# Convolution taps accumulated in a PSUM bank that the attention's side work shares, in a hybrid encoder block

## The chip, the cores and the metric

The kernel runs on one core of a Trainium2 chip. The metric is the time of one execution on the device in microseconds (us), the median of several runs. Engines are named as in the profile: PE multiplies matrices, DVE is the vector engine, ACT the scalar engine, POOL the GpSimd engine, SP issues DMAs. Each engine works through its own queue in program order. SBUF is the large on-chip memory; PSUM is the small one that PE writes into, 8 banks of 512 fp32 columns on 128 partitions.

## What is computed

The input is 1024 tokens of 1024 channels, all fp32. Cut to what matters here:

```python
h = rmsnorm(x, norm1_g); p = h @ w_in            # q | k | v | value | gate
q, k = rope(rmsnorm(q)), rope(rmsnorm(k))        # 8 query heads, 2 key heads, 64 wide
attn = softmax(q k^T / 8) v
c = value * sigmoid(gate)                        # 512 channels
c = depthwise_conv(c, conv_dw, width=31) + conv_b
conv = silu(layernorm(c))
x = x + concat(attn, conv) @ w_out
out = rmsnorm(x + peer(rmsnorm(x)))              # 16384 experts, top 16 of 8 heads
```

## The kernel before

Everything up to the output projection takes the first 591 us and is what the change touches; the expert part (`peer`) fills the rest of the span and is untouched. An order written out by hand (`manual_schedule`) fixes each engine's queue: instructions run on an engine in the order in which the Python code emits them. Matrix products are made of three products of split operands (`split` on L114, `mm3` on L121: the high part is cast on ACT, the low part is a subtraction on DVE or POOL).

**Stage A** (to L484) makes Q, K, V and the gated convolution input `hp`. The convolution's 512 channels are four tiles c of 128 channels; the 1024 tokens are two halves th. For each (c, th), `ag_mm` (L252) makes the gate (k=1) and then the value (k=0), each 24 matmuls into one half of a PSUM tile of two banks, of which there are two; `ag_sg` (L260) applies the sigmoid on ACT, and `ag_mul` (L265) writes the product into `hp` on DVE. The other four banks (tag `t`) serve the transposes and the projections of K, V (`kv_mm`) and Q (`q_mm`). The order is c = 3, then 0 and 1, then K and V for eight token tiles, Q for eight token tiles, then c = 2.

**The taps.** The convolution has 31 taps. A pass takes one tile c and 512 tokens: a first step multiplies by the first tap and adds the bias, and 30 more steps add one tap each. On DVE (`taps_v`, L141) a step is one instruction that reads `hp` shifted by w, multiplies by the tap's column and adds to `y`, in place in SBUF. On POOL (`taps_p`, L149) a step multiplies into a tile `cm` (on ACT in stage A, on POOL in the attention, switch `alone`) and adds it to `y`. The passes are generators in two queues, `ct_v` and `ct_p`; `adv(n)` emits the next n steps. The places of these calls and the constants CV1 to CV3, CP1, CP3, AV0, AV1, AP0, AP1 set how many taps stand between the other instructions. DVE takes the passes of tiles 3 and 1 and the second half of 2, POOL those of tile 0 and the first half of 2.

**The attention** (L492 to L816) has 64 units, one for each of 8 token tiles and 8 heads. The loop on L761 emits for each unit u, in the order of ORD: both halves of the transposed probabilities (`p_tr`, tile ptP, split into PT), the next exponential (`s_exp`), scores two units ahead (`s_mm`) and their maximum (`s_max`, L697, one per unit: it serves as the unit's clock), every fourth unit the transposed queries (`qt_make`, ql and qh), every second unit the product with V (`pv`) and the fold and scaling (`pfold`, L741 to L744, into `mo`). Then come taps of both queues.

Side work goes into slots of this loop: when the 8 heads of a token tile are done, its output projection (`outproj`, L590) is queued: 4 transposes, a split, and for each half of the columns 12 + 12 matmuls and an addition to X, 8 steps in all. When all passes of a token half are done, its layernorm (`layernorm_steps`, L506) is queued, and goes first. `slot("c")`, `slot("p")` and `slot("q")` each emit the current item's next step if it is of that kind; one item is worked on at a time, and all of them use one PSUM bank (`side_bank`, tag `x`). What is left at the end of the loop is emitted behind it (L803 to L815), step by step without other work, and then `outproj_conv` (L607) adds the convolution's part: PE products pwo<-PT and additions on L616.

Of the kernel before, what the change touches and what calls it, by code (L numbers as in the profile page):

```python
# [53 lines left out]
AV1 = 2  # L54
AV0 = 1
# [7 lines left out]
CP1 = 3  # L63
CP3 = 2
AP1 = 1
AP0 = 2
CV1 = 6
CV2 = 3
CV3 = 6


def peer_block(tc, I, out):
# [54 lines left out]
    with ExitStack() as fr:  # L127
# [10 lines left out]
        cm_ = fr.enter_context(tc.tile_pool(name="cm", bufs=1))  # L138
        hp = [None] * NCT

        def taps_v(c, o):  # L141
            yo = y[c][:, o:o + 512]
            V.tensor_scalar(yo, hp[c][:, o:o + 512], cw[:, c, 0:1], cvec[:, 0, c:c + 1], op0=ALU.mult, op1=ALU.add)
            yield
            for w in range(1, CW):
                V.scalar_tensor_tensor(yo, hp[c][:, w + o:w + o + 512], cw[:, c, w:w + 1], yo, op0=ALU.mult, op1=ALU.add)  # L146
                yield

        def taps_p(c, o):  # L149
            yo = y[c][:, o:o + 512]  # L150
            G.tensor_scalar(yo, hp[c][:, o:o + 512], cw[:, c, 0:1], cvec[:, 0, c:c + 1], op0=ALU.mult, op1=ALU.add)
            yield
            for w in range(1, CW):
                m = cm_.tile([P, 512], F32, name="cm", tag="cm", bufs=2)
                src = hp[c][:, w + o:w + o + 512]
                if alone["on"]:
                    G.tensor_scalar(m[:], src, cw[:, c, w:w + 1], 0.0, op0=ALU.mult, op1=ALU.add)
                else:
                    A.activation(m[:], src, AF.Copy, scale=cw[:, c, w:w + 1])
                G.tensor_tensor(yo, yo, m[:], op=ALU.add)  # L160
                yield

        alone = dict(on=False)
# [17 lines left out]
        left = {(c, o) for c in range(NCT) for o in (0, 512)}  # L181

        with ExitStack() as st:
# [68 lines left out]
            def ag_mm(c, th, k):  # L252
                if k == 1:
                    PA[c, th] = ps.tile([P, 2, 512], F32, name="pa", tag="big", bufs=2)
                w = WAG[k * NCT + c]
                for dc in range(DC):
                    mm3(PA[c, th][:, k, :], w[0][:, dc, :], w[1][:, dc, :],
                        hT(0, dc, th * 512, 512), hT(1, dc, th * 512, 512), dc == 0, dc == DC - 1)

            def ag_sg(c, th):  # L260
                sg = y[2][:, th * 512:(th + 1) * 512]
                A.activation(sg, PA[c, th][:, 1, :], AF.Sigmoid)
                PA[c, th] = (PA[c, th], sg)

            def ag_mul(c, th):  # L265
                pa, sg = PA.pop((c, th))
# [4 lines left out]
                V.tensor_tensor(hp[c][:, PAD + th * 512:PAD + (th + 1) * 512], pa[:, 0, :], sg, op=ALU.mult)  # L271
# [104 lines left out]
            ag_mm(3, 0, 1)  # L376
            prep_b(4)
# [5 lines left out]
            ag_sg(3, 0)  # L383
# [4 lines left out]
            ag_mm(3, 1, 1)  # L388
            wsplit_ag(4, G)
            ag_mm(3, 1, 0)  # L390
            ag_sg(3, 1)
# [3 lines left out]
            for o in (0, 512):  # L395
                ct_v.add(taps_v(3, o), (3, o))
            for c in (0, 1):
                for th in range(2):
                    for k in (1, 0):
# [7 lines left out]
                        ct_v.adv(1)  # L407
                        if k == 0:
                            ag_sg(c, th)
                            ag_mul(c, th)  # L410
                        ct_v.adv(CV1 - 1)
                        ct_p.adv(CP1 - th)
                WAG.pop(c), WAG.pop(c + 4)
                if c == 0:
                    for o in (0, 512):
                        ct_p.add(taps_p(0, o), (0, o))
                else:
                    ct_v.add(taps_v(1, 0), (1, 0), True)
                    ct_v.add(taps_v(1, 512), (1, 512))
# [27 lines left out]
            for t in range(NT):  # L447
# [6 lines left out]
                else:  # L454
                    qa(t - 1)
                    ct_v.adv(CV2)
                if t == 1:
# [10 lines left out]
            for th in range(2):  # L468
                for k in (1, 0):
# [6 lines left out]
                    if k == 0:  # L476
                        ag_sg(2, th)
                        ag_mul(2, th)
                    if th == 0 or k == 1:
                        ct_v.adv(CV3)  # L480
                    if th == 0:
                        ct_p.adv(CP3)
            ct_p.add(taps_p(2, 0), (2, 0), True)
            ct_v.add(taps_v(2, 512), (2, 512))  # L484
# [7 lines left out]
        with ExitStack() as st:  # L492
# [3 lines left out]

            def side_bank(name):
# [1199 lines left out]
```

## Time and profile before

| | us |
|---|---|
| runs of the kernel | 3000.25, 3005.8, 3015.49 |
| median | 3005.8 |
| the profiled execution | 3001.72 |
| its span, first to last instruction | 2999.9 |

The profiled execution's time is that of the whole execution; its span is 1.8 us shorter. In the rows below, a tile is named without its buffer number, out<-in; "x5" is a number of instructions merged into one row, and the time of such a row runs from the first one's start to the last one's end. The releaser in brackets is inferred, and "issue" means that the profile shows none. `L119` and `L122` to `L124` are lines of the helpers `split` and `mm3`, so the tile's name says what they work for.

### The profile page before, as it was taken

The numbers are of one execution on the slowest core, as the hardware profiler recorded it, in microseconds if no ns is written. First come the engines' busy times: TensorE is split into PE (matmuls) and PEld (weight loads), VectorE is DVE, ScalarE is ACT, GpSimd is POOL, SyncE is SP. The second block draws the span as 40 slices with busy tenths as digits, with TensorE's granted clock in tenths as the row PEclk, the third lists the DMA queues.
The fourth block names the chain that finished last, engine by engine and source line by source line (L and its number), as shares of the span: only waits on it lengthen the run. The fifth ranks groups of instructions, "written<-read, shape, count | busy, mean of one in ns | idle before, by whom it ended". The sixth has DMA issues, their size and how long they took to land.

```text
span 2999.9 us, 44538 instructions
## 1 busy us (share of the span) xinstructions
PE 2796.1 (93%) x16048; PEld 2476.5 (83%) x16048; DVE 2464.3 (82%) x4465; ACT 1148.3 (38%) x2376; POOL 1951.2 (65%) x1557
## 2 busy tenths in 40 slices
PE   7878899899999899988999999999999999999997
PEld 6767778699978788867888888888888888888886
DVE  5888998457667867874999988898999999899898
ACT  3216566243577577673222222222222222222222
POOL 2577842104445757774777777777777777777775
PEclk9999999999999999999999999999999999999999
DMA  3111000044334567576889898999899999999896
GB/s 125 51 68 36 8 1 15 31 145 131 109 122 163 205 245 265 196 288 246 340 330 344 328 347 334 339 337 355 335 338 335 354 342 340 339 339 340 331 343 230
DMA packets 296720, 710.33 MB, mean 237 GB/s; under 512 B 25265, under 2 KB 135217, under 8 KB 296369
## 3 DMA queue, kind: packets, MB, share of 16 engines
q0 software_dynamic: 110592, 402.70, 35.1%
q1 hardware_dynamic: 156800, 252.85, 25.0%
q10 hardware_dynamic: 29104, 51.91, 4.6%
q8 instruction: 126, 2.06, 0.3%
q14 instruction: 98, 0.79, 0.1%
HBM read 640.46 MB, written 66.91 MB: 236 GB/s over the span
## 4 chain that ended last, share of the span: by engine, by line
PE 50%; DVE 21%; DMA 12%; issue 8%; POOL 4%; ACT 4%; ACTq 1%; SPq 0%; POOLq 0%; DVEq 0%
PE hps L1492 12%; PE hps L1234 5%; PE prot L122 4%; PE prot L123 3%; PE prot L124 3%; DMA rows<-peer_u,ei 3%; DMA vr<-peer_v 3%; DVE y L146 3%; PE pg L1098 3%; DMA rows<-peer_v,ei 3%; DVE ga L1197 2%; PE acc L122 2%; PE acc L124 2%; PE acc L123 2%; DVE ho L1475 2%
## 5 line engine op out<-in xcount | busy, mean ns | idle before, releaser
L1492 PE MATMUL hps<-HN,uh 128*128 128x320 f32 x3072 | 682.9, 310 | 9.9 <-ACT ho L1241 5.3
L1492 PEld LDWEIGHTS hps<-HN,uh 128*128 128x128 f32 x3072 | 530.3, 188 | 42.9 <-issue 5.5
L1492 PE MATMUL hps<-HN,ul 128*128 128x320 f32 x1536 | 476.1, 310 | 0.6 <-POOL ul L119 0.6
L1197 DVE SCALAR_TENSOR_TENSOR ga<-rows,aa,ga 128x1024 f32<-128x1024 f32 x330 | 423.9, 1285 | 23.3 <-DMA rows<-peer_v,ei 16.7
L1152 POOL DMA_INDIRECT rows<-peer_u,ei x339 | 360.3, 1063 | 109.5 <-issue 57.9
L119 POOL TENSOR_TENSOR vl<-vr,vh 128x1024 fp32r<-128x1024 f32 x128 | 308.9, 2413 | 154.0 <-ACT vh L116 110.8
L1152 POOL DMA_INDIRECT rows<-peer_v,ei x330 | 325.4, 986 | 110.6 <-issue 64.1
L1185 DVE SCALAR_TENSOR_TENSOR QB<-rows,ga 128x1024 bf16<-128x1024 f32 x271 | 329.5, 1216 | 30.0 <-DMA rows<-peer_u,ei 25.8
L122 PE MATMUL prot<-vh,ah 128*128 128x512 f32 x762 | 308.3, 405 | 29.2 <-DVE X L1557 26.9
L119 POOL TENSOR_TENSOR ul<-ur,uh 128x1024 fp32r<-128x1024 f32 x127 | 323.2, 2545 | 2.6
L1557 DVE TENSOR_TENSOR X<-X,prot 128x512 f32<-128x512 f32 x384 | 262.0, 682 | 68.1 <-PE prot L124 66.7
L123 PE MATMUL prot<-vl,ah 128*128 128x512 f32 x762 | 301.2, 395 | 0.4 <-POOL vl L119 0.4
L124 PE MATMUL prot<-vh,al 128*128 128x512 f32 x762 | 297.6, 390 | 0.0
L1492 PEld LDWEIGHTS hps<-HN,ul 128*128 128x128 f32 x1536 | 289.2, 188 | 0.9 <-POOL ul L119 0.9
L1502 ACT ACTIVATE ho<-hps 128x320 f32<-128x320 f32 x128 | 55.8, 436 | 486.4 <-PE hps L1492 486.4
L1108 ACT COPY gblk<-pg 128x128 f32<-128x128 f32 x640 | 175.9, 441 | 97.0 <-PE pg L1098 72.5
L116 ACT CAST vh<-vr 128x1024 fp32r<-128x1024 f32 x128 | 133.7, 1045 | 202.1 <-DMA vr<-peer_v 193.3
L1234 PE MATMUL hps<-HN,uh 128*128 128x320 f32 x992 | 210.0, 334 | 0.0
L124 PE MATMUL acc<-vh,al 128*128 128x512 f32 x512 | 199.6, 390 | 0.0
L122 PE MATMUL acc<-vh,ah 128*128 128x512 f32 x512 | 199.6, 390 | 0.0
L123 PE MATMUL acc<-vl,ah 128*128 128x512 f32 x512 | 199.5, 390 | 0.0
L122 PEld LDWEIGHTS prot<-vh,ah 128*128 128x128 f32 x762 | 143.3, 188 | 64.6 <-DVE X L1557 44.5
(270 smaller groups left out, 6556.6 us busy)
## 6 DMA issues: line engine op xcount, KB each, us to landing
ur<-peer_uT SPq DMA_DIRECT2D x128, 512.0 KB, 4.2
vr<-peer_v SPq DMA_DIRECT2D x128, 512.0 KB, 7.8
GD<-gblk ACTq DMA_DIRECT2D x80, 512.0 KB, 5.2
gl<-GD SPq DMA_DIRECT2D x64, 640.0 KB, 8.0
wqr<-peer_wq SPq DMA_DIRECT2D x32, 512.0 KB, 3.9
HDm<-ho SPq DMA_DIRECT2D x31, 320.0 KB, 2.6
s<-SD SPq DMA_DIRECT2D x64, 128.0 KB, 2.9
ho<-HDm SPq DMA_DIRECT2D x22, 320.0 KB, 4.6
```

The source lines that it names most:

```text
L116: A.copy(hi, src)
L119: lo_eng.tensor_tensor(lo, src, f(hi), op=ALU.subtract)
L122: PE.matmul(ps, ah, bh, start=start, stop=False)
L123: PE.matmul(ps, ah, bl, start=False, stop=False)
L124: PE.matmul(ps, al, bh, start=False, stop=stop)
L1108: A.copy(gblk[b][k][:, :, q * 4:q * 4 + 4].rearrange("p i t -> p t i"), pg[:, :, k * w:k * w + w])
L1152: G.indirect_dma_start(out=r, out_offset=None, in_=I["peer_v" if ph else "peer_u"], in_offset=bass.IndirectOffsetOnAxis(ap=ge[t][:, k:k + ...
L1185: V.scalar_tensor_tensor(jk, r, 1.0, h, op0=ALU.mult, op1=ALU.mult, accum_out=self.hh[t][:, k:k + 1])
L1197: V.scalar_tensor_tensor(to, r, self.aa[t][:, k:k + 1], to, op0=ALU.mult, op1=ALU.add)
L1234: PE.matmul(hps[:, j, :b - a], (uh, uh, ul)[st3][:, dc, :], HN[(0, 1, 0)[st3]][:, dc, a:b], start=dc == 0 and st3 == 0, stop=dc == DC - 1 ...
L1492: PE.matmul(ps[:, :b - a], (uh, uh, ul)[st3][:, dc, :], HN[(0, 1, 0)[st3]][:, dc, a:b], start=dc == 0 and st3 == 0, stop=dc == DC - 1 and ...
L1557: V.tensor_tensor(X[:, NG + t, n:n + 512], X[:, NG + t, n:n + 512], pr, op=ALU.add)
```

## The change

The taps of DVE accumulate in a PSUM tile `ac` instead of `y`; only the last tap writes `y`. The bank for it comes from a new pool `psT` that lives through stage A and the attention, and it is the bank of the side work (layernorm and output projection). In stage A the gate and the value each get a bank of their own, three in rotation, in place of two tiles of two banks; the sigmoid is emitted right behind the gate's matmuls. POOL multiplies and adds its taps alone everywhere, none on ACT. The second half of tile 0 is divided: tokens 512 to 767 stay on POOL, 768 to 1023 go to DVE. The numbers of steps per place change. In the attention each unit gets two steps of each queue; the slots take up no side work until DVE's queue of taps is empty, and from then on, while more than one item waits, the order ORD2 gives a unit two "p" and two "c" slots. The result of a unit goes into the columns of Q that it has used, not into a tile of its own.

```diff
@@ -51,8 +51,8 @@
 ORD = "c01esmdqvpf"
-AV1 = 2
-AV0 = 1
+ORD2 = "c01pesmdcqvpf"
+AV0 = 2
 GQ = 4
@@ -60,13 +60,13 @@
 RH = 4
-CP1 = 3
-CP3 = 2
-AP1 = 1
+CP1 = 2
+CP2 = 1
+CP3 = 1
 AP0 = 2
-CV1 = 6
-CV2 = 3
-CV3 = 6
+CV1 = 7
+CV2 = 4
+CV3 = 5
@@ -136,31 +136,31 @@
         cm_ = fr.enter_context(tc.tile_pool(name="cm", bufs=1))
+        psT = fr.enter_context(tc.tile_pool(name="psT", bufs=1, space=PSUM))
         hp = [None] * NCT
-        def taps_v(c, o):
-            yo = y[c][:, o:o + 512]
-            V.tensor_scalar(yo, hp[c][:, o:o + 512], cw[:, c, 0:1], cvec[:, 0, c:c + 1], op0=ALU.mult, op1=ALU.add)
+        def side_bank(name):
+            return psT.tile([P, 512], F32, name=name, tag="x", bufs=1)
+        def taps_v(c, o, n=512):
+            yo = y[c][:, o:o + n]
+            ac = side_bank("ac")[:, :n]
+            V.tensor_scalar(ac, hp[c][:, o:o + n], cw[:, c, 0:1], cvec[:, 0, c:c + 1], op0=ALU.mult, op1=ALU.add)
             yield
             for w in range(1, CW):
-                V.scalar_tensor_tensor(yo, hp[c][:, w + o:w + o + 512], cw[:, c, w:w + 1], yo, op0=ALU.mult, op1=ALU.add)
+                V.scalar_tensor_tensor(ac if w < CW - 1 else yo, hp[c][:, w + o:w + o + n], cw[:, c, w:w + 1], ac,
+                                       op0=ALU.mult, op1=ALU.add)
                 yield
-        def taps_p(c, o):
-            yo = y[c][:, o:o + 512]
-            G.tensor_scalar(yo, hp[c][:, o:o + 512], cw[:, c, 0:1], cvec[:, 0, c:c + 1], op0=ALU.mult, op1=ALU.add)
+        def taps_p(c, o, n=512):
+            yo = y[c][:, o:o + n]
+            G.tensor_scalar(yo, hp[c][:, o:o + n], cw[:, c, 0:1], cvec[:, 0, c:c + 1], op0=ALU.mult, op1=ALU.add)
             yield
...
                 m = cm_.tile([P, 512], F32, name="cm", tag="cm", bufs=2)
-                src = hp[c][:, w + o:w + o + 512]
-                if alone["on"]:
-                    G.tensor_scalar(m[:], src, cw[:, c, w:w + 1], 0.0, op0=ALU.mult, op1=ALU.add)
-                else:
-                    A.activation(m[:], src, AF.Copy, scale=cw[:, c, w:w + 1])
-                G.tensor_tensor(yo, yo, m[:], op=ALU.add)
+                G.tensor_scalar(m[:, :n], hp[c][:, w + o:w + o + n], cw[:, c, w:w + 1], 0.0, op0=ALU.mult, op1=ALU.add)
+                G.tensor_tensor(yo, yo, m[:, :n], op=ALU.add)
                 yield
-        alone = dict(on=False)
@@ -178,7 +178,12 @@
         ct_v, ct_p = Steps(), Steps()
-        left = {(c, o) for c in range(NCT) for o in (0, 512)}
+        left = set()
+        def taps(q, fn, c, o, n=512, front=False):
+            left.add((c, o))
+            q.add(fn(c, o, n), (c, o), front)
@@ -250,25 +255,24 @@
             def ag_mm(c, th, k):
-                if k == 1:
-                    PA[c, th] = ps.tile([P, 2, 512], F32, name="pa", tag="big", bufs=2)
+                PA[c, th, k] = ps.tile([P, 512], F32, name="pa", tag="big", bufs=3)
                 w = WAG[k * NCT + c]
                 for dc in range(DC):
-                    mm3(PA[c, th][:, k, :], w[0][:, dc, :], w[1][:, dc, :],
+                    mm3(PA[c, th, k][:], w[0][:, dc, :], w[1][:, dc, :],
                         hT(0, dc, th * 512, 512), hT(1, dc, th * 512, 512), dc == 0, dc == DC - 1)
...
                 sg = y[2][:, th * 512:(th + 1) * 512]
-                A.activation(sg, PA[c, th][:, 1, :], AF.Sigmoid)
-                PA[c, th] = (PA[c, th], sg)
+                A.activation(sg, PA.pop((c, th, 1))[:], AF.Sigmoid)
+                PA[c, th] = sg
             def ag_mul(c, th):
-                pa, sg = PA.pop((c, th))
+                pa, sg = PA.pop((c, th, 0)), PA.pop((c, th))
                 if th == 0:
...
                     V.memset(hp[c][:, PAD + T:], 0.0)
-                V.tensor_tensor(hp[c][:, PAD + th * 512:PAD + (th + 1) * 512], pa[:, 0, :], sg, op=ALU.mult)
+                V.tensor_tensor(hp[c][:, PAD + th * 512:PAD + (th + 1) * 512], pa[:], sg, op=ALU.mult)
@@ -374,26 +378,26 @@
             ag_mm(3, 0, 1)
+            ag_sg(3, 0)
             prep_b(4)
...
             prep_a(7)
-            ag_sg(3, 0)
             prep_b(6)
...
             ag_mm(3, 1, 1)
+            ag_sg(3, 1)
             wsplit_ag(4, G)
             ag_mm(3, 1, 0)
-            ag_sg(3, 1)
             wsplit_ag(0, G)
...
             for o in (0, 512):
-                ct_v.add(taps_v(3, o), (3, o))
+                taps(ct_v, taps_v, 3, o)
             for c in (0, 1):
@@ -404,19 +408,20 @@
                             wsplit_q("q", 1 - k, (V, G)[k])
-                        ct_v.adv(1)
                         if k == 0:
+                            ag_mul(c, th)
+                        else:
                             ag_sg(c, th)
-                            ag_mul(c, th)
-                        ct_v.adv(CV1 - 1)
-                        ct_p.adv(CP1 - th)
+                        ct_v.adv(CV1)
+                        ct_p.adv(CP1)
                 WAG.pop(c), WAG.pop(c + 4)
                 if c == 0:
-                    for o in (0, 512):
-                        ct_p.add(taps_p(0, o), (0, o))
+                    taps(ct_p, taps_p, 0, 0)
+                    taps(ct_p, taps_p, 0, 512, 256)
                 else:
-                    ct_v.add(taps_v(1, 0), (1, 0), True)
-                    ct_v.add(taps_v(1, 512), (1, 512))
+                    taps(ct_v, taps_v, 1, 0)
+                    taps(ct_v, taps_v, 1, 512)
+                    taps(ct_v, taps_v, 0, 768, 256)
@@ -454,6 +459,7 @@
                     ct_v.adv(CV2)
+                    ct_p.adv(CP2)
                 if t == 1:
@@ -474,14 +480,14 @@
                     if k == 0:
+                        ag_mul(2, th)
+                    else:
                         ag_sg(2, th)
-                        ag_mul(2, th)
                     if th == 0 or k == 1:
                         ct_v.adv(CV3)
-                    if th == 0:
                         ct_p.adv(CP3)
-            ct_p.add(taps_p(2, 0), (2, 0), True)
-            ct_v.add(taps_v(2, 512), (2, 512))
+            taps(ct_p, taps_p, 2, 0)
+            taps(ct_v, taps_v, 2, 512)
@@ -493,9 +499,6 @@
             st.enter_context(tc.manual_schedule())
-            def side_bank(name):
-                return ps.tile([P, 512], F32, name=name, tag="x", bufs=1)
@@ -589,15 +592,15 @@
                 yield "p"
-                pt = ps.tile([P, 4, P], F32, name="pmT", tag="x", bufs=1)
+                pt = side_bank("pmT")[:].rearrange("p (a b) -> p a b", a=4)
                 for j in range(4):
...
                 mT = mixed()
-                split(mT[0][:], mT[1][:], pt[:])
+                split(mT[0][:], mT[1][:], pt)
                 for n0 in (0, 512):
                     yield "p"
-                    po = ps.tile([P, 512], F32, name="pwo", tag="x", bufs=1)
+                    po = side_bank("pwo")
                     mms(po[:], mT, 0, n0, (0, 1))
@@ -654,7 +657,7 @@
                 if it is None:
-                    if not pend and not convq:
+                    if ct_v.q or not pend and not convq:
                         return
@@ -735,7 +738,7 @@
                 if h == 0:
-                    mo_[t] = b_.tile([P, NH, HD], F32, name="mo", tag="mo", bufs=2)
+                    mo_[t] = Q[:, t, :].rearrange("p (h d) -> p h d", d=HD)
                 fo = op[:, 2 * P:].rearrange("p (h d) -> p h d", d=HD)
@@ -744,7 +747,7 @@
                     mo = mo_.pop(t)
-                    pend.append(outproj(t, mo[:].rearrange("p a b -> p (a b)")))
+                    pend.append(outproj(t, mo.rearrange("p a b -> p (a b)")))
@@ -783,20 +786,15 @@
                         slot("c")
-                for ch in ORD:
-                    r = parts(ch)
-                    if ch == "p":
-                        busy = r
-                alone["on"] = True
-                ct_p.adv(AP1 if busy else AP0)
-                alone["on"] = False
+                for ch in (ORD2 if len(pend) + len(convq) > 1 and not ct_v.q else ORD):
+                    parts(ch)
+                ct_p.adv(AP0)
                 if u in (1, 3, 5, 7):
                     wo_split(u // 2)
-                if not convq and not aux:
-                    ct_v.adv(AV1 if busy else AV0)
+                ct_v.adv(AV0)
                 aux_adv()
                 for th in range(2):
-                    if side["ln"] == th and not any(o == th * 512 for _, o in left):
+                    if side["ln"] == th and not any(o // 512 == th for _, o in left):
                         convq.append(layernorm_steps(th))
...
```

## Rows read from the trace of the kernel before

**Rows 1.** Windows: us, busy us (instructions) of PE, PEld, DVE, ACT, POOL, PE clock, DMA.
```profile
108.00:124.00 16.00, 3.49 (x27) 3.32 (x27) 13.79 (x33) 0.48 (x3) 5.42 (x10) 0.71 0.17 49
...
208.00:225.50 17.50, 0.00 (x0) 0.00 (x0) 16.85 (x20) 1.21 (x3) 12.04 (x9) 0.57 0.69 270
...
255.00:275.00 20.00, 17.71 (x103) 15.47 (x104) 18.08 (x26) 13.46 (x25) 19.41 (x17) 0.84 0.18 53
```

**Rows 2.** Waits of PE, 100 to 235 us: total us, times, longest us.
```profile
PE ptq L677 <- issue: 18.0, 1, 18.0
PE pk L342 <- DVE kd L339: 15.2, 3, 12.5
```

**Rows 3.** Timeline of DVE, stage A: start us, us, operation, count, [idle before].
```profile
56.39 0.69 DVE L271 TENSOR_TENSOR hp<-pa,y 128x512 f32<-128x512 f32 x1 [9.98 <-ACT y L262]
...
113.55 3.90 DVE L146 SCALAR_TENSOR_TENSOR y<-hp,cw,y 128x512 f32<-128x512 f32 x5
...
200.46 9.23 DVE L146 SCALAR_TENSOR_TENSOR y<-hp,cw,y 128x512 f32<-128x512 f32 x6
...
210.25 14.24 DVE L146 SCALAR_TENSOR_TENSOR y<-hp,cw,y 128x512 f32<-128x512 f32 x12
...
224.56 0.68 DVE L271 TENSOR_TENSOR hp<-pa,y 128x512 f32<-128x512 f32 x1
```

**Rows 4.** Timeline of POOL: Q stage, then two steps of a tap.
```profile
163.85 0.63 POOL L104 TENSOR_SCALAR rp<-ss 128x8 f32<-128x8 f32 x1 [1.44 <-DVE ss L307]
...
184.37 2.15 POOL L105 TENSOR_TENSOR rs<-rp,mhalf 128x8 f32<-128x8 f32 x1
...
192.57 1.29 POOL L323 TENSOR_TENSOR h<-h,rope 128x512 f32<-128x512 f32 x1
193.94 1.31 POOL L324 TENSOR_TENSOR Q<-h,t 128x512 f32<-128x512 f32 x1
...
266.31 1.28 POOL L160 TENSOR_TENSOR y<-y,cm 128x512 f32<-128x512 f32 x1
267.57 0.69 POOL L157 TENSOR_SCALAR cm<-hp,cw 128x512 f32<-128x512 f32 x1
```

**Rows 5.** Timeline of DVE in the attention.
```profile
234.77 1.22 DVE L697 TENSOR_REDUCE mx<-S 128x1 f32<-128x1024 f32 x1
...
370.61 0.67 DVE L119 TENSOR_TENSOR ql<-ptq,qh 128x512 fp32r<-128x512 f32 x1
...
371.70 1.53 DVE L146 SCALAR_TENSOR_TENSOR y<-hp,cw,y 128x512 f32<-128x512 f32 x2
373.15 1.28 DVE L119 TENSOR_TENSOR PT<-ptP,PT 128x512 fp32r<-128x512 f32 x2
374.35 1.21 DVE L697 TENSOR_REDUCE mx<-S 128x1 f32<-128x1024 f32 x1
...
439.63 1.22 DVE L697 TENSOR_REDUCE mx<-S 128x1 f32<-128x1024 f32 x1
...
497.90 1.21 DVE L697 TENSOR_REDUCE mx<-S 128x1 f32<-128x1024 f32 x1
...
516.64 1.22 DVE L697 TENSOR_REDUCE mx<-S 128x1 f32<-128x1024 f32 x1
```

**Rows 6.** A line's instructions: count, ns least/median/most, first and last start, form.
```profile
L605 DVE TENSOR_TENSOR X<-X,pwo x16: 673/682/690, 289.2 to 546.5; 128x512 f32<-128x512 f32 x16
L560 DVE SCALAR_TENSOR_TENSOR y<-th,y x8: 681/684/1141, 428.9 to 532.7; 128x512 f32<-128x512 f32 x8
```

**Rows 7.** Timeline of PE, the last two output projections.
```profile
526.25 0.66 PE L594 MATMUL pmT<-ident,mo 128*128 128x128 f32 x4
...
535.99 0.66 PE L594 MATMUL pmT<-ident,mo 128*128 128x128 f32 x4 [0.78 <-DVE X L605]
...
546.05 0.39 PE L124 MATMUL pwo<-wo,mT 128*128 128x512 f32 x1
546.28 0.39 PE L122 MATMUL pwo<-PT,mT 128*128 128x512 f32 x1
```

## The prediction

> **What bounds the kernel now.** The change touches only the first 591 us of the span; the expert part behind is the same code and starts when the last output projection is added, so I ask how far that moment moves. I read the stages first (windows), then whom PE waits for, then the queue of the engine it waits for.
>
> PE is busy nearly throughout, with two holes. Between 108 and 124 us it works 3.49 of 16 us, and from 208 to 225.5 us not at all [rows 1]. The waits name the first: transposes of K wait 12.5 us for DVE's copy kd [rows 2], which is queued behind taps that end at 113.55 + 3.90 = 117.4 us [rows 3]. The second is put down to "issue" [rows 2]; DVE's queue explains it [rows 3]. Six taps run from 200.46 us, twelve from 210.25 us, and only at 224.56 us comes the product hp<-pa that frees stage A's last bank; it ends at 225.2, and 0.3 us later PE's first transpose of stage B starts. These taps show the cost that the change attacks: twelve take 14.24 us, 1.19 each, with POOL at work beside them, while five with POOL idle take 3.90 us, so 0.74 for one and (3.90 - 0.74) / 4 = 0.79 start to start in a chain.
>
> In the attention DVE is the bound while it has taps. The unit up to the maximum at 374.35 us shows it without a gap [rows 5]: ql and the fold 371.70 - 370.61 = 1.09, two taps 1.45, two splits 1.20, the maximum 1.13 (1.21, overlapped by 0.08). The fold (0.49) comes every second unit, ql (0.60) every fourth, so a unit costs DVE 1.20 + 1.13 + 0.25 + 0.15 = 2.73 us before taps.
>
> **The change part by part.** The numbers of steps follow from the code: before, DVE has five passes of 31 steps (155) and POOL three (93). After, DVE has five full passes and one over 256 columns (186), POOL two full and one over 256 (93).
>
> *A tap on PSUM.* No row shows DVE writing PSUM. Nearest are its operations with one operand there: X<-X,pwo takes 0.68 us, as does y<-th,y with both in SBUF when POOL is quiet (minimum 0.681) [rows 6]. The latter reaches 1.14 at worst, the former never passes 0.69. So I take 0.74 alone and 0.79 in a chain, undisturbed by POOL. Bounds: below, streaming alone, since 512 columns more cost 1.21 - 0.68 = 0.53 [rows 5, 6]; above, the disturbed 1.19.
> [...]
>
> *Gate and value in single banks.* A group's bank is wanted again three groups later, and its reader has two groups of matmuls for it, as before: 0. ACT's sigmoid moves in front of the value's matmuls. At the earlier place ACT waits for the gate anyway, and at the old one the chain over the last normalised rows ends last: 0; below, a gain of the sigmoid's own 2 us or less.
>
> *Stage A, gate and value groups.* Before 48 taps, now 56, seven per group. DVE starts with the product of 56.39 us [rows 3], 0.8 earlier because the sigmoid is done: 55.6 + 0.7. Then 56 x 0.79 = 44.2, a wait for the first value group of 4.7 (its two groups are 48 products at 0.23 [rows 7], DVE's first seven taps half of that), three more products and four weight splits, some 7.5: about 113 instead of 117.4 us. Gain 4.
>
> *Stage A, Q.* POOL sets the pace here. A tile is a small operation of 0.6, the power 2.15, and two rope operations of 1.29 and 1.31 [rows 4], with gaps 5.6 us if DVE does not disturb. The change gives POOL one tap in each of seven tiles, with no help from ACT: 0.69 + 1.28 + gaps = 2.05, so 7.65 a tile. The third tile's small operation starts at 163.85 - 4 = 159.9; five tiles on it is 198.1, its power is done at 200.9, the rope operations of the tile before at 203.6, DVE's last rope operation at 204.1 us, against 200.46 where the six taps start now. Behind it DVE has 5 + 5 + 5 taps and two products, 15 x 0.79 + 1.3 = 13.1 us, instead of 24. So the last product ends at 217.2 instead of 225.2: **stage A gains 8 us** (4 to 12). ACT loses its part of POOL's taps. DMA issues keep their places.
>
> *Attention, first part.* 86 of DVE's steps are left, two per unit: 43 units, and the queue is seen empty in the next. Until then the slots start nothing, since the accumulator holds the side bank; before, three and a half output projections and one layernorm were done by then. A unit with two full taps costs 2.73 + 1.45 = 4.18, one over 256 columns about 3.67 (0.74 - 0.27 = 0.47 each, chained 0.52). 27.5 x 4.18 + 15.5 x 3.67 + one of 3.1 = 175, and 0.1 per unit for small gaps: 179 us from the first unit's maximum to that of the 45th. Before: 439.63 - 234.77 = 204.9 [rows 5]. POOL has 75 taps and four weight splits, some 141 us, and delays nothing; the casts, transposes and scores hide under DVE. **26 us ahead**, 34 with stage A, with the side work undone.
>
> *Attention, second part.* Twenty units remain, PE the bound. The four from 497.90 to 516.64 us hold a layernorm's heavy half: 4.69 each [rows 5]; I take 4.5 for the mean of a layernorm's 7 units, 63 us for two layernorms. Then the doubled slots: an output projection is 24 products at 0.23 and four transposes, 6.1 us of PE, and some 3.1 of its 8 steps fall in a unit, 2.4. A bare unit is (58.3 - 2.5 x 6.1) / 13 = 3.3 (58.3 from 439.63 to 497.90, with 2.5 projections). Four units at 5.7 make 23; two without scores 9.5; the last four hold 12 steps in a row, 16. Together 111.5: the loop ends at 234.8 - 8 + 179 + 111.5 = 517.3 us.
>
> *Tail.* By count, projections 4 to 7 and the last addition of 3 are left, where now it is half of 6 and 7. All use one bank, so each step waits for the one before: 535.99 - 526.25 = 9.74 us from transposes to transposes, and 11 for the next (last product at 546.05 us, its addition 0.68) [rows 6, 7]. 4 x 10.2 + 1 = 42. The convolution's products start at 559.3 instead of 546.28 us: **13 us later**. Behind them every instruction is as before.
>
> Writing a unit's result into Q, in place of a tile of its own, costs 0: those columns of Q have been read long before.
>
> Sum: -8 - 26 + 47 for what was put off = +13 on the profiled execution (3001.7 us, span 2999.9), which lies 4.1 under the median of 3005.8. So **3019 us**, own range 3007 to 3031 (stage A 4 either way, DVE's units 5, slots and tail 6).
>
> **The rivals.**
> *A chain on PSUM waits longer: slower than before.* Place: between two taps, where one waits for the other's result, now 0.79 - 0.74 = 0.05. If that wait is paid two or three times over, 71 taps of stage A and 86 of the attention cost 0.055 to 0.11 more each: 8.6 to 17 us, 3028 to 3036. It decides from 0.015 per tap on, which takes 3019 past 3021. For it: DVE has not written PSUM yet. Against it: the equal rows. [...]
> *Taps that do not wait: faster.* If a chain on PSUM ran at the 0.60 of independent operations (the two splits, 1.20 [rows 5]), stage A's groups would end 11 us and the attention's pairs 10 us earlier: 2998; at the streaming bound of 0.53, 2989. Against it: a tap needs the result before it.
> *PE's clock: slower.* In the first part PE would work 3.2 of 4.2 us. The granted clock was 0.57 from 208 to 225.5 us, with PE idle, and 0.84 from 255 to 275 us, with DVE the bound [rows 1]. [...]
> *The change doesn't do what it says:* POOL disturbs a tap on PSUM as before, 1.19. Then 55 x 0.45 + 31 x 0.27 = 33 in the attention, stage A's 8 and 8 more: 3068. Against it: X<-X,pwo stays at 0.68 whatever POOL does.
>
> **How the numbers follow.** A measurement tells 0.5%, 15 us, from no change. Forecast 0.56; +13 lies close to the bound, so 0.33 of it stays below and 0.23 goes over. Longer wait 0.12, clock 0.07, still disturbed 0.05, all slower. No wait 0.20, of which 0.11 past -15 and 0.09 not. Slower 0.23 + 0.12 + 0.07 + 0.05 = 0.47; same 0.33 + 0.09 = 0.42; faster 0.11. The range goes from a little under the 2998 of the case without wait, 2994, to the clock's 3045; outside lie the deeper part of that case, the disturbed taps and half of the clock, under 2 in 10. The forecast's own range is 3007 to 3031.
>
> **What would show it.** Right, if the taps on the new accumulator last 0.73 to 0.76; PE's hole ends near 217 us; no layernorm product and no pmT before the taps are done; the maxima of the first 43 units lie 4.2 and 3.7 us apart; the tail shows eight pwo additions 5 us apart; the products pwo<-PT start near 559 us. A step is wrong if taps last over 0.85 or stretch beside POOL, if PE and not DVE paces the first part, or if a projection of the tail takes under 9 us. The whole is wrong if pwo<-PT starts before 546 us.

## The result and the profile after

The changed kernel takes 3024.97 us, the median of 7 runs (3019.5 to 3027.52), and the kernel before 3001.83 us, the median of 7 runs that now include the three shown above. The ratio is 1.0072, with a 95% interval of 1.006 to 1.0085: slower by 23 us. The profiled execution has a span of 3024.1 us, against 2999.9. The time is lost ahead of the expert part: the last addition X<-X,pwo of 1024 columns starts at 612.0 instead of 590.8 us, 21 us later; of the rest, 3 us, nothing is told here, since runs of one kernel differ by more.

Stage A first. Waits of PE in the changed kernel from 100 to 235 us (total us, times, longest us), which answer to [rows 2]:

```profile
PE pk L346 <- DVE kd L343: 10.7, 4, 7.5
PE ptq L680 <- issue: 7.6, 1, 7.6
PE pq L285 <- DVE h L320: 2.8, 1, 2.8
```

Timeline of DVE in the changed kernel, stage A and the first unit, against [rows 3, 5]:

```profile
54.14 0.69 DVE L275 TENSOR_TENSOR hp<-pa,y 128x512 f32<-128x512 f32 x1 [10.61 <-PE pa L124]
...
105.30 5.50 DVE L151 SCALAR_TENSOR_TENSOR ac<-hp,cw,ac 128x512 f32<-128x512 f32 x7
110.71 0.35 DVE L305 TENSOR_TENSOR rope<-rope,gq 128x64 f32<-128x64 f32 x2
...
201.04 3.91 DVE L151 SCALAR_TENSOR_TENSOR ac<-hp,cw,ac 128x512 f32<-128x512 f32 x5
...
213.33 0.68 DVE L275 TENSOR_TENSOR hp<-pa,y 128x512 f32<-128x512 f32 x1
...
224.52 1.23 DVE L700 TENSOR_REDUCE mx<-S 128x1 f32<-128x1024 f32 x1 [0.40 <-PE S L693]
225.66 1.54 DVE L151 SCALAR_TENSOR_TENSOR ac<-hp,cw,ac 128x512 f32<-128x512 f32 x2
```

The wait for "issue" went from 18.0 to 7.6 us, the one for kd from 15.2 to 10.7. Taps still stand ahead of the last product hp<-pa, but they no longer stretch: five from 201.04 us take 3.91, as five with POOL idle took 3.90 before [rows 3]. POOL is at work beside them this time. Windows (us, busy us (instructions) of PE, PEld, DVE, ACT, POOL, granted clock, DMA share, GB/s) of the changed kernel and, in the second fence, of the kernel before:

```profile
201.00:205.00 4.00, 4.00 (x19) 3.31 (x18) 3.86 (x9) 0.60 (x1) 3.59 (x4) 1.00 0.00 0
```

```profile
113.50:117.40 3.90, 0.00 (x0) 0.00 (x0) 3.76 (x7) 0.00 (x0) 0.00 (x0) 0.66 0.54 174
```

The last product starts 11.2 us earlier, 213.33 against 224.56, and the first unit's maximum 10.25 us, 224.52 against 234.77.

All taps of the changed kernel, by line (count, ns least/median/most, first and last start, form). L148 is a pass's first step, L151 the other thirty, of which the last writes `y` and is not in the first row:

```profile
L151 DVE SCALAR_TENSOR_TENSOR ac<-hp,cw,ac x174: 478/756/757, 55.6 to 394.3; 128x512 f32<-128x512 f32 x145, 128x256 f32<-128x256 f32 x29
...
L148 DVE TENSOR_SCALAR ac<-hp,cw,cvec x6: 536/814/815, 54.8 to 332.7; 128x512 f32<-128x512 f32 x5, 128x256 f32<-128x256 f32 x1
```

Of 145 taps over 512 columns none takes more than 0.757 us, also where POOL is busy for 41.18 of 45 us (228 to 273 us). In this the change did what it was meant to do.

The attention, timeline of DVE: the last units with taps, and then single maxima (one per unit):

```profile
390.48 1.54 DVE L151 SCALAR_TENSOR_TENSOR ac<-hp,cw,ac 128x512 f32<-128x512 f32 x2
391.93 1.28 DVE L119 TENSOR_TENSOR PT<-ptP,PT 128x512 fp32r<-128x512 f32 x2
393.13 1.22 DVE L700 TENSOR_REDUCE mx<-S 128x1 f32<-128x1024 f32 x1
...
402.10 1.23 DVE L700 TENSOR_REDUCE mx<-S 128x1 f32<-128x1024 f32 x1 [2.31 <-PE S L693]
...
436.66 1.22 DVE L700 TENSOR_REDUCE mx<-S 128x1 f32<-128x1024 f32 x1 [3.52 <-PE S L693]
...
477.29 1.23 DVE L700 TENSOR_REDUCE mx<-S 128x1 f32<-128x1024 f32 x1 [1.72 <-PE S L693]
...
497.94 1.22 DVE L700 TENSOR_REDUCE mx<-S 128x1 f32<-128x1024 f32 x1 [1.48 <-PE S L693]
```

Look at the idle times in brackets: with taps DVE runs almost without a gap (busy for 87.71 of the 90 us from 310 to 400 us), and from the 45th unit (402.10 us) on it waits for scores. The first layernorm fills the units from 402.10 to 436.66 us (7, so 4.94 each), the second those to 477.29 us (7, so 5.80), and the doubled slots with projections take 20.65 us for the three units to 497.94 (6.88 each).

The tail, timeline of PE in the changed kernel, against [rows 7], and below it the additions by line (columns as above):

```profile
528.13 0.66 PE L597 MATMUL pmT<-ident,Q 128*128 128x128 f32 x4 [1.01 <-DVE X L608]
...
537.81 0.66 PE L597 MATMUL pmT<-ident,Q 128*128 128x128 f32 x4 [0.78 <-DVE X L608]
...
547.51 0.66 PE L597 MATMUL pmT<-ident,Q 128*128 128x128 f32 x4 [0.78 <-DVE X L608]
...
558.65 0.66 PE L597 MATMUL pmT<-ident,Q 128*128 128x128 f32 x4 [0.78 <-DVE X L608]
...
567.38 0.39 PE L122 MATMUL pwo<-PT,mT 128*128 128x512 f32 x1
```

```profile
L608 DVE TENSOR_TENSOR X<-X,pwo x16: 674/687/690, 485.2 to 567.6; 128x512 f32<-128x512 f32 x16
L619 DVE TENSOR_TENSOR X<-X,pwo x8: 1214/1215/1222, 574.8 to 612.0; 128x1024 f32<-128x1024 f32 x8
```

No projection is added before 485.2 us (289.2 before, [rows 6]), four whole ones are left for the tail, and the convolution's products start at 567.38 instead of 546.28 us, 21 us later.

### The profile page after: what moved, and what is told of

Read it like the earlier page. It is cut to its first block, busy times and chain, and to the rows that moved or that the text cites. A ratio compares the mean times of both kernels' runs of the same rounds, so it can differ in the third digit from the quotient of the medians.

```text
span 3024.1 us, 44553 instructions
## 1 busy us (share of the span) xinstructions
PE 2808.3 (93%) x16042; PEld 2480.5 (82%) x16048; DVE 2421.5 (80%) x4496; ACT 1140.5 (38%) x2363; POOL 1902.2 (63%) x1570
## 4 chain that ended last, share of the span: by engine, by line
PE 53%; DVE 21%; DMA 9%; issue 7%; ACT 5%; POOL 4%; ACTq 1%; another core or an unknown queue 0%; SPq 0%; POOLq 0%; DVEq 0%
PE hps L1490 14%; PE hps L1232 5%; PE prot L122 4%; PE prot L123 4%; PE prot L124 4%; DMA rows<-peer_u,ei 3%; DVE ac L151 3%; PE pg L1096 3%; PE acc L123 2%; PE acc L124 2%; PE acc L122 2%; DMA vr<-peer_v 2%; DVE PT L119 2%; DVE mx L700 2%; DVE ho L1473 2%
```

## The experiments

The theory in all of them: taps in PSUM are a gain wherever nobody else wants the bank, and the loss is made in the attention, where one bank serves the taps and the side work, so that the side work is put off into crowded units and a tail. Medians of the kernel before moved between 2997.6 and 3002.6 us over the runs, so ratios to it are compared, with 95% intervals in brackets; one thousandth is 3 us.

### Stage A of the change with the attention of before

The edit against the changed kernel, cut where dots stand:

```diff
+        def taps_v(c, o, n=512, bank=True):
+            ac = side_bank("ac")[:, :n] if bank else yo
...
-                    taps(ct_v, taps_v, 1, 512)
-                    taps(ct_v, taps_v, 0, 768, 256)
+                    taps(ct_v, taps_v, 1, 512, bank=False)
...
-                    if ct_v.q or not pend and not convq:
+                    if not pend and not convq:
...
-                ct_v.adv(AV0)
+                if not convq and not aux:
+                    ct_v.adv(AV1 if busy else AV0)
```

with CV3 = 3, the order ORD throughout, AV1, AV0 and AP1 of before, POOL's passes of before, and pass (2, 512), that is tile 2 and the tokens from 512 on, in SBUF too.

> Stage A as in the changed kernel (three passes of VectorE in PSUM, single banks, early sigmoid); the attention as before the change (accumulators in SBUF, side work not held back, split of the passes between VectorE and GpSimd as before). Theory, that stage A gains 10 us and the attention loses 34 by holding its side work back: the Q stage ends some 14 us before the old 225.2 us (six taps fewer than in the changed kernel at its end), the attention then runs as of old, the last addition of X<-X,pwo (1024 columns) starts near 577 instead of 590.8 us, and the total is 2988 us (2983 to 2994), faster than both. Rival, that taps in SBUF beside GpSimd are what the attention cannot bear: it gives the gain of stage A back, 3002 or later.

Measured: 2989.35 us, ratio 0.9954 (0.9936 to 0.9972). The last product hp<-pa starts at 207.33 us, the last addition of 1024 columns at 575.5 us. Faster than both kernels, as the theory had it: what the change lost, it lost in the attention.

### The same, with the side work held back

The edit against the run above:

```diff
-                    if not pend and not convq:
+                    if ct_v.q or not pend and not convq:
...
+                for ch in (ORD2 if len(pend) + len(convq) > 1 and not ct_v.q else ORD):
```

and two steps of both queues in every unit, where the run above takes at most two.

> As the run above, but the side work waits until VectorE's taps are done, two taps in every unit, doubled slots behind, as in the changed kernel; accumulators of the attention stay in SBUF. Theory, that putting the side work off is the loss: TensorE works some 3.3 of 4.9 us in 31 units, the 50 us that it then lacks come back behind, the total is 30 to 50 us over the run above, about 3030. Rival, that the loss of the changed kernel comes from the accumulator's place or from VectorE's larger share of the taps: within 10 us of the run above.

Measured: 3042.67 us, ratio 1.0138 (1.0115 to 1.0161), 53 us over the run above, a little past the theory's range. Windows of this kernel (us, busy us of PE, PEld, DVE, ACT, POOL, granted clock, DMA share, GB/s) and, in the second fence, of the changed kernel:

```profile
275.00:325.00 50.00, 40.30 (x237) 35.40 (x237) 49.16 (x61) 26.49 (x50) 48.25 (x44) 0.84 0.04 11
```

```profile
275.00:325.00 50.00, 43.01 (x306) 37.75 (x305) 48.73 (x86) 35.75 (x67) 47.41 (x64) 1.00 0.04 11
```

Both are bound by DVE. With taps in SBUF it does 61 instructions in the 50 us, in PSUM 86, but its taps in that stretch are the short ones of 256 columns. A fair comparison is from 228 to 273 us, where both add 512 columns and POOL is busy for over 40 of the 45 us: a tap takes 1.62 us in SBUF and 0.75 in PSUM. Taps there, by form (count, busy us, mean ns, idle before), in this kernel and then in the changed one:

```profile
L151 DVE SCALAR_TENSOR_TENSOR y<-hp,cw,y 128x512 f32<-128x512 f32 x15 | 24.3, 1620 | 0.2
```

```profile
L151 DVE SCALAR_TENSOR_TENSOR ac<-hp,cw,ac 128x512 f32<-128x512 f32 x20 | 15.0, 752 | 0.3
```

From 275 to 325 us PE is granted 0.84 of the clock instead of 1.00. So the condition of the rival from PE's clock, which did not come in the changed kernel, shows here; but DVE, busy for 49.16 of the 50 us, stays the bound.

The 53 us are not the price of putting off alone. This kernel's first 30 units hold only attention and taps, and take 161.3 us (maxima from 218.74 to 380.00); the run above, with side work in its units, takes 137.4 (218.05 to 355.42). So 24 us are lost where the taps stand closer and stretch, and 31 from there to the last addition (631.1 against 575.5 us; the first unit is 0.7 later). No run puts the side work off in SBUF without packing the taps closer.

### Scores ahead of the first side step

The changed kernel with `ORD2 = "c01esmpdcqvpf"` for `"c01pesmdcqvpf"`.

> The changed kernel, but in the doubled order the first side step of TensorE is put behind the scores instead of ahead of them. Theory, that the units of the layernorms last 5.4 instead of 4.5 us because a side product (two-column products of 1.95 to 3.41 us, or a product waiting for its diagonal) stands ahead of the scores on TensorE: maxima of those units some 4.9 apart, total 6 us under the changed kernel, 3019 (3014 to 3022). Rival, that the sum of TensorE's work at the granted clock (0.83 from 440 to 480 us) sets them: the same as the changed kernel within 2 us.

Measured: 3013.57 us, ratio 1.0038 (1.0021 to 1.0054), so 0.0034 or 10 us under the changed kernel. PE in the changed kernel, around the first two-column products of the second layernorm:

```profile
446.65 0.87 PE L719 MATMUL ptP<-ident,Pm 128*128 128x128 f32 x4 [0.84 <-DVE ql L119]
447.31 3.41 PE L534 MATMUL pv<-ones,csq 128*128 128x2 f32 x16
450.59 0.78 PE L692 MATMUL S<-KP,qh 128*128 128x512 f32 x1
...
452.44 2.68 PE L731 MATMUL ot<-PT,VV 128*128 128x256 f32 x16
```

and the same place in this kernel:

```profile
445.04 0.48 PE L692 MATMUL S<-KP,qh 128*128 128x512 f32 x1
...
446.06 1.84 PE L534 MATMUL pv<-ones,csq 128*128 128x2 f32 x16
447.76 2.17 PE L731 MATMUL ot<-PT,VV 128*128 128x256 f32 x16
```

In the first the scores stand 3.4 us behind the transposes, and the maximum, the exponential and the next transposes stand behind them; in the second they follow at once. The layernorm units are 5.09 us apart (398.75 to 470.00 for 14) instead of 5.37, the step into the first of them is 2.79 instead of 5.20, and the three doubled units 18.16 instead of 20.65. So the place of the step is a part of it, larger in the end than expected, though the layernorm units themselves stay above the 4.9 of the theory. PE's clock is not the same in the two rows of products above (see the last section), so in these units the place and the clock are not parted by this run.

### The tail's projections in other banks

```diff
-                    po = side_bank("pwo")
+                    po = ps.tile([P, 512], F32, name="pwo", tag="pt", bufs=2) if late else side_bank("pwo")
...
             wo_conv()
+            late.append(1)
```

> The changed kernel, but the output projections behind the last unit take their product banks from the two of the transposes, which are free by then, instead of the one shared bank. Theory, that the tail is a chain over one bank: a projection takes 7.6 instead of 9.7 us (transposes, a wait of 1.5 for the split, 24 products), four of them save 8 us, 3017 (3013 to 3021). Rival, that the tail is bound by something else (the split on ScalarE and VectorE, the additions): 3025.

Measured: 3017.05 us, ratio 1.0049 (1.0031 to 1.0066), 0.0023 or 7 us under the changed kernel. PE in this kernel:

```profile
536.84 0.60 PE L597 MATMUL pmT<-ident,Q 128*128 128x128 f32 x4
...
543.96 0.60 PE L597 MATMUL pmT<-ident,Q 128*128 128x128 f32 x4
...
551.07 0.60 PE L597 MATMUL pmT<-ident,Q 128*128 128x128 f32 x4
...
558.16 0.39 PE L122 MATMUL pwo<-PT,mT 128*128 128x512 f32 x1
```

A projection takes 7.1 us instead of 9.7, and the wait for the addition ahead of it (0.78 us) is gone. The chain over one bank is what set the tail.

### Single banks and the early sigmoid alone

The edit against the kernel before:

```diff
-                if k == 1:
-                    PA[c, th] = ps.tile([P, 2, 512], F32, name="pa", tag="big", bufs=2)
+                PA[c, th, k] = ps.tile([P, 512], F32, name="pa", tag="big", bufs=3)
...
                         if k == 0:
-                            ag_sg(c, th)
                             ag_mul(c, th)
+                        else:
+                            ag_sg(c, th)
```

> The kernel before with single banks for gate and value and the sigmoid ahead of the value's products, and nothing else of the change. Theory, that the 10 us of stage A come from taps that GpSimd no longer stretches: 3000 to 3003, the last product hp<-pa of stage A within 2 us of 224.6 us. Rival, that banks and sigmoid carry part of the gain: 2997 or less, and the wait of K's transposes for kd well under the 15.2 us of before.

Measured: 3001.07 us, ratio 1.0004 (0.9993 to 1.0015): no gain that can be told. In its profile DVE's first product starts at 54.34 us (56.39 before, [rows 3]), the last at 222.13 us (224.56 before), which is 2.4 us instead of the 2 allowed, and PE waits as before:

```profile
PE ptq L678 <- issue: 17.3, 1, 17.3
PE pk L341 <- DVE kd L338: 15.3, 3, 12.5
```

So of the changed kernel's 10.25 us in stage A some 2 may be the sigmoid's, and the rest comes with the taps; the last experiment tells their place from their order.

### The attention's accumulators in SBUF

The changed kernel with `bank=False` for DVE's passes (0, 768), the one over 256 columns, and (2, 512).

> The changed kernel, but VectorE's last two passes (62 of its 86 steps in the attention, half of them of 256 columns) accumulate in SBUF; side work held back and doubled slots as in the changed kernel. Theory, that PSUM does help in the attention, since GpSimd stretches taps in SBUF there too: the 45th unit starts some 10 us later, total 3035 (3029 to 3040). Rival, that the attention has slack on VectorE and the place does not matter: 3025.

Measured: 3045.78 us, ratio 1.015 (1.0131 to 1.017), 0.0078 or 23 us over the changed kernel, twice the expectation. The first 44 units take 194.7 us (224.87 to 419.53) instead of 177.6 (224.52 to 402.10). Taps of DVE in this kernel, 225 to 330 us, grouped by form (count, busy us, mean ns, idle before):

```profile
L151 DVE SCALAR_TENSOR_TENSOR y<-hp,cw,y 128x256 f32<-128x256 f32 x25 | 20.6, 824 | 0.5
L151 DVE SCALAR_TENSOR_TENSOR ac<-hp,cw,ac 128x512 f32<-128x512 f32 x23 | 17.3, 751 | 0.4
```

Half the columns in SBUF take longer (0.824, from 276 us on) than all of them in PSUM (0.751, up to 273 us). In the changed kernel POOL, which has the same two steps per unit there, is busy for 41.18 of the 45 us from 228 to 273 us and for 47.41 of the 50 from 275 to 325 us. In PSUM the short taps take 0.485 in the changed kernel. Of the 17 us by which the 45th unit is later, 12.6 lie in the units with the short taps (274.62 to 346.14 us, against 275.73 to 334.61).

### The fourth pass in PSUM too, and the tail's banks with it

The first experiment's kernel (the edit is against it) with pass (1, 512) in PSUM, CV3 = 5, two taps per unit and the side work held back only while that pass holds the bank:

```diff
-                    if not pend and not convq:
+                    if held or not pend and not convq:
...
-                    ct_v.adv(AV1 if busy else AV0)
+                    ct_v.adv(2 if held else AV1 if busy else AV0)
```

> The first experiment's kernel, but the fourth pass stays in PSUM too: 7 of its taps at the end of stage A as in the changed kernel, 24 in the first 12 units, two in each; the side work is held back only until that pass ends, about when the first output projection is ready. Theory, that taps are cheap in PSUM as long as no side work wants the bank: 12 taps of 1.1 us fewer stand in the later units, 3 us more in the first ones, total 2984 (2979 to 2989). Rival, that TensorE sets the later units: as the first experiment, 2989.

> The kernel of the run above, with the projections behind the last unit in the two banks of the transposes. One and a half projections are left there: 3 us under the run above by the theory (2.1 each), the same if the tail is not a chain over the shared bank any more.

Measured: 2983.81 us, ratio 0.9945 (0.9929 to 0.996), and with the tail's banks 2985.62 us, ratio 0.9946 (0.993 to 0.9963). The first lies where the theory put it, but its interval overlaps that of the first experiment, so the gain over it is not shown; the other banks for a tail of one and a half projections bring nothing that can be told. All three, the first experiment's with them, beat the kernel before by about 0.5% and the changed one by 1.2%.

### Both repairs of the changed kernel's second part

The scores first and the tail's projections in the banks of the transposes, in the changed kernel.

> The changed kernel with both repairs of its second part: scores ahead of the first side step, and the tail's projections in the banks of the transposes. Theory, that the two terms lie behind one another and add up (11 and 8 us measured one by one), and that what is left of the loss is the side work put off: 3006 (3001 to 3011), the kernel before to within what a measurement tells, and still some 17 us over the first experiment's 2989. Rival, that they are the whole of the loss by the side work: 2995 or less.

Measured: 2996.84 us, ratio 0.9999 (0.9987 to 1.0012): the kernel before, as expected by ratio, though 9 us lower in us than the number written (the kernel before measured 2997.57 in these runs). Together they bring 0.0073, or 22 us, where one by one they brought 10 and 7; the 5 us beyond the sum lie within the intervals and are not explained. It remains 0.0045, 13 us, over the first experiment, a difference in which the gain of the attention's taps in PSUM is already taken off. The rival, that the two repairs are the whole of the loss, would have come out at 2995 or less, 0.9975 by ratio: it falls.

### Stage A of the change without PSUM

The first experiment's kernel with `bank=False` for all passes.

> The first experiment's kernel with all of VectorE's passes in SBUF: the order of work of the changed stage A without PSUM accumulators. Theory, that the accumulator's place is what stage A gains by: taps there last some 1.05 on the mean of stage A as before, 94 x 0.3 = 28 us more of VectorE of which the cover of TensorE takes the larger part, the last product hp<-pa of stage A comes near 223 us again, total 3003 (2998 to 3012). Rival, that the order (seven taps per group, GpSimd's steps one per tile, fewer taps at the end) brings the gain: 2989.

Measured: 3010.85 us, ratio 1.0039 (1.0024 to 1.0053), against 0.9954 with the accumulators in PSUM: 0.0085, or 25 us, for the place alone. Taps of this kernel from 60 to 225 us, by form, and below them all its taps (columns as for L151 and L608 above):

```profile
L153 DVE SCALAR_TENSOR_TENSOR y<-hp,cw,y 128x512 f32<-128x512 f32 x83 | 82.9, 998 | 2.4
...
L153 DVE SCALAR_TENSOR_TENSOR y<-hp,cw,y x150: 734/753/2960, 58.3 to 476.2; 128x512 f32<-128x512 f32 x150
```

In stage A they take 1.00 us each instead of 0.756, the last product hp<-pa starts at 234.59 us, 27 us behind the first experiment's 207.33 and later than the 223 expected, and PE waits 17.8 us for kd. The changed order of stage A (seven taps a group, POOL's taps spread over the Q tiles without ACT's help) is by itself no gain: in SBUF it ends 10 us behind the kernel before. It pays only with the accumulators in PSUM.

## Why the prediction was right, and which term was off

The direction and the mechanism came out as forecast: 3019 against a kernel before of 3005.8, so 1.0044, and 3025 against 3001.8, so 1.0072, measured. The size was too small: 13 us later were forecast for the products pwo<-PT, 21 were measured, and 1.0044 lies under the measured interval. By its own steps:

- *A tap on PSUM:* 0.74 alone and 0.79 in a chain were forecast; 0.756 and (5.50 - 0.756) / 6 = 0.79 were measured, pairs 1.54. Nothing of POOL's work shows in them: none over 512 columns passed 0.757. Taps still disturbed, the last rival, and taps that do not wait fell here. So did the longer wait: 0.756 stands against 0.751 for the mean of the five with POOL idle [rows 3], and the chain's pitch did not move (0.79).
- *Stage A:* 8 forecast, 11.2 measured at the last product and 10.25 at the first unit's maximum. The groups gained 6.7 (110.71 against 117.4) instead of 4. Of this 2.25 is the first product's earlier start (54.14 against 56.39), forecast as 0.8 and, in the part on the banks, taken as 0.
- *Attention, first part:* 179 forecast, 402.10 - 224.52 = 177.6 measured. This is the step where everything was read from DVE's rows, and it held.
- *Attention, second part:* this is the mis-sized term. The 14 units of the layernorms were put at 4.5 each, 63 us, from four units of before that took 4.69 with a layernorm in single slots [rows 5]; they took 477.29 - 402.10 = 75.2. In the changed kernel the doubled order holds for them too (projections are queued behind them, so more than one item waits), and it puts a side step of PE ahead of the scores. With it moved behind them, 4 us of the 12 went away in those units, 2.4 in the step into them and 2.5 in the doubled units behind. Of the 4, 3.6 fall to the second layernorm's units, where the granted clock rose too, from 0.84 to 0.91, so that the place alone is not shown to bring them. Of the other 8 some 2 go with PE's clock. The run with both repairs has the same work up to the last unit as the run with the scores first; in its profiled execution the second layernorm's units were granted 1.00 of the clock instead of 0.91 and took 34.9 instead of 37.0 us. Windows of the run with both repairs and, in the second fence, of the one with the scores first:

```profile
397.73:431.99 34.26, 32.65 (x217) 28.32 (x216) 25.04 (x44) 21.87 (x53) 4.25 (x6) 0.95 0.00 1
431.99:466.85 34.86, 30.37 (x212) 25.76 (x211) 27.33 (x49) 23.74 (x56) 4.80 (x6) 1.00 0.01 1
```

```profile
432.97:470.00 37.03, 33.15 (x212) 28.18 (x211) 27.34 (x49) 23.77 (x56) 4.80 (x6) 0.91 0.00 1
```

At the nearly full clock the 14 units take 69.1 us, of which PE is busy for 63.0, as long as the forecast gave to the units altogether. The 6 us in which PE is not busy had no place in it; they are not told apart further.
- *From there to the tail and in it:* 49.5 us forecast to the first transposes of the tail (the four doubled units, two without scores, the last four and the last addition: 23 + 9.5 + 16 + 1), 528.13 - 477.29 = 50.8 measured; four projections at 10.2 make 40.8, and 567.38 - 528.13 = 39.3 was measured.

The sum: 2 us more from stage A and 1 each from the first part and the tail, against 12 from the layernorms and 1 behind them, make 8 or 9: the products pwo<-PT start at 567.4, not 559.3 us. So the term of the layernorms alone was off by more than the whole sum was. PE's clock, as a rival for the first part, did not come: 1.00 was granted from 275 to 325 us, with DVE the bound. No run shows the term of the clock behind the 3045 us at which the range ends: in the run with the side work held back, with 0.84 granted in the same stretch, DVE was the bound too (busy for 49.16 of the 50 us).

What the prediction had as one sum, a gain of 34 us ahead and a loss of 47 behind, the experiments split. PSUM is worth 25 us in stage A and 23 in the attention, each in the order of work of the changed kernel; against the kernel before, with its own order, stage A of the change gains 14 (0.9954). The side work put off and the taps packed closer cost 53 us with taps in SBUF, 31 of them behind the first 30 units. With taps in PSUM, the change is 0.0118 or 35 us slower than the first experiment, which differs from it in the attention and in six taps at the end of stage A; the 23 are already gained back in that. Of these 35 the two repairs take 22, which were the tail on one bank and the place ahead of the scores, and leave 13.

## What to carry to other kernels

A bank that takes an accumulator out of a contended memory (a tap took 1.62 us in SBUF and 0.75 in PSUM, with POOL busy) pays as long as no other work of that stage is waiting for it: price the holding of the bank by what must wait for it, and where that has to run alone later, at what it costs there and not where it ran hidden. When postponed work is fitted into doubled slots, keep the producer of the critical chain (here the scores, which brought 10 us) ahead of it on the in-order queue. A change with a good and a bad half is worth taking apart: here the first half alone was 0.5% faster, the whole 0.7% slower.

## What was not expected of the hardware

- How completely the place of one operand decides. A tap reads `hp` from SBUF in either case; with the accumulator in SBUF too it ran from 0.73 to 2.96 us in the last experiment, with it in PSUM 512 columns never passed 0.757.
- A pass's first step, a tensor_scalar with one tensor operand, is the one that became dearer: 0.81 us into PSUM, where it took 0.54 into SBUF at 54.95 us of the kernel with single banks alone. There are six of them, so it matters little here.
- The granted clock fell to 0.50 of full speed from 448 to 452 us of the changed kernel, while PE was busy throughout; ahead of that, from 444 to 448 us, it had worked 2.84 of 4 us. With the scores first it worked 3.37 us in that earlier window and 1.00 was granted in both. The 16 two-column products took 3.41 us in the one case and 1.84 in the other.
